# Decode step on one core: in the sample attention, a chunk's four transposes ahead of its score products, and seven load buffers

## The chip, the cores and the metric

The kernel is one program on one core of a Trainium2 chip. The metric is the device time of an execution in microseconds (us). The engines are TensorE (PE, with its weight loads as PEld), VectorE (DVE), ScalarE (ACT), GpSimd (POOL) and SyncE (SP). Here SP only issues DMA transfers, and POOL issues the gathers.

## The reference, cut to what matters

The program is one step of a hybrid layer for two groups that share all weights: a prompt of 1024 tokens and 8 samples of 4 new tokens with a past of 2048. The part that the change is about is the attention of the samples:

```python
def nsa_block(q, g, pos_q, ck, cv, kb, vb, kw, vw, pos_w):
    s = einsum(q, ck) * scale - slope * d_c          # compressed blocks
    o_c = masked_probs(s) @ cv
    _, idx = top_k(score, 16)                        # blocks of 64 rows
    ks, vs = kb[idx], vb[idx]                        # selected blocks
    o_s = masked_probs(einsum(q, ks) * scale - slope * d_s) @ vs
    o_w = masked_probs(einsum(q, kw) * scale - slope * d_w) @ vw   # last 512 rows
    return gate[0] * o_c + gate[1] * o_s + gate[2] * o_w

def memory_attend(mq, mkv):                          # 256 memory rows, 4 heads
    return softmax(mq @ k * scale) @ v

def merge(x, o_a, o_b, o_c, gb, w_o):
    return x + (concatenate([o_a, o_b, o_c]) * gb) @ w_o
```

Everything before and after it (projections, the prompt's own attention, the state space branch, the MLP) is the same in both kernels.

## The kernel before, in words

`run` (L129) builds the program in stages. The instructions of a stage are written in program order, and a scheduler in the framework then fixes the order on every engine before the program runs. It lays the stages over one another where tiles and buffers allow. On the chip each engine takes its instructions strictly in that order.

Three stages matter here. `nsa_keys` (L695) makes the prompt's keys: it loads `kd` and transposes it into `kps` (L735), loads the bias rows `augk` on POOL's queue (L725 to L727) and the rows `augq` on SP's (L705). `sample` (L1322) is the attention of the samples, and `nsa_prompt` (L741) the attention of the prompt. The last two run over one another on all engines: `sample` has the PSUM tag `sS` with two banks, `nsa_prompt` has `S` (three banks, the scores, L835 to L838), `T` (two, transposed probabilities, L889) and `O` (one, L903). For a unit of the prompt, `prep` (L774) makes QB on POOL from `augq` (L786). DVE finds the maximum of each score tile (L843) and scales the probabilities (L876); ACT takes the exponential (L844) and copies T out of PSUM (L891).

`sample` goes twice (Q = 0, 1) over four samples each. In each round it first scores the compressed blocks and ranks the blocks on DVE and POOL (L1446 to L1455). Then come five chunks: the window (c = 4) and the four quarters of the selected blocks (c = 0 to 3). A chunk needs four tiles `xs` (128x1024 f32, one per sample). For the window SP loads them; for the other chunks they are gathered by POOL's queue from `cache_slc_kv` (L1334). There are six `xs` buffers, so that while a chunk holds four, the next one can have two on the way. A chunk's steps are a product that puts the bias into its score bank S (L1489); for each of four groups a: four transposes of the keys (L1494), an evacuation to SBUF on ACT or DVE (L1343, L1345) and four score products (L1498); the maximum and the exponential (L1501, L1507); four transposes of the probabilities (L1517); and sixteen value products (L1523), after which the four `xs` are free. S is held all the while, so the transposes of a chunk have the other bank of `sS` alone. After the chunks a round ends with the memory part: eight tiles of keys and values from `cache_mem_kv` through the same `xs` buffers (L1332), eight groups of transposes and products (L1563, L1567), value products (L1584) and the gated result in `mixs`.

After both, `out_proj` (L1637) multiplies the mixed branches with `w_o` (L122 to L124 on `ops`), in the order of the tuple `ORDER = (4, 5, 6, 0, 7, 1, 8, ...)` of feature blocks. Blocks 4 to 11 are loaded from scratch (`mxr`), and split into a high and a low part on ACT and DVE (L112 `mxh`, L118 `mxl`). Their tiles lie in the SBUF space that `sample` leaves, and so can be made once it is done. The first weight block `w0` is loaded and split early, during `nsa_prompt`; the others (`raw` <- `w_o`, L1624) lie in the space that `nsa_prompt` and its keys leave.

Of the kernel before, what the change touches and what calls it, by code (L numbers as in the profile page):

```python
# [8 lines left out]
F32 = mybir.dt.float32  # L9
R32 = mybir.dt.float32r  # L10
BF16 = mybir.dt.bfloat16
# [3 lines left out]
ALU = mybir.AluOpType  # L15
# [86 lines left out]
class Build:  # L102
# [593 lines left out]
    def nsa_keys(self, pool):  # L696
        nc, A = self.nc, self.A
# [6 lines left out]
        self.augq = pool.tile([128, 1032], F32, name="augq")  # L704
        nc.sync.dma_start(self.augq[64:128], A["c_augq"])  # L705
# [64 lines left out]
    def nsa_units(self, pool, psp, j, g):  # L770
        nc = self.nc
        ctx = {"n": 0, "total": (j + 1) + min(j + 1, 5) + 1}

        def prep():  # L774
            tk = slice(j * 128, j * 128 + 128)
            qd = pool.tile([128, 4, 128], F32, name="qd", tag="qd", bufs=3)
            for dd in range(2):
                nc.sync.dma_start(qd[dd * 64:(dd + 1) * 64], self.s_q[g * 256:(g + 1) * 256, tk].rearrange("(h d) t -> d h t", d=64))
            qd = qd.rearrange("p h t -> p (h t)")
            if g == 0:  # L780
                self._gn = pool.tile([128, 3, 8], F32, name="gn", tag="gn", bufs=2)
                nc.sync.dma_start(self._gn.rearrange("p b h -> p (b h)"), self.s_gn[tk])
            ctx["gn"] = self._gn
            QA = pool.tile([128, 512], R32, name="QA", tag="QA", bufs=2)
            QB = pool.tile([128, 512], R32, name="QB", tag="QB", bufs=2)
            nc.gpsimd.tensor_scalar(QB[64:128], self.augq[64:128, g * 512:(g + 1) * 512], self.augq[64:128, 1024 + j:1025 + j], None, op0=ALU.mult)  # L786
            nc.scalar.activation(QA, qd, AF.Copy, scale=0.125)
            nc.vector.scalar_tensor_tensor(QB[0:64], qd[0:64], 0.125, QA[0:64].bitcast(F32), op0=ALU.mult, op1=ALU.subtract)
            ctx["QA"], ctx["QB"] = QA, QB
            ctx["gb"] = pool.tile([128, 256], F32, name="ngb", tag="ngb", bufs=5)  # L790
            for a in range(2):
                nc.sync.dma_start(ctx["gb"][:, a * 128:(a + 1) * 128], self.s_gb[2 * g + a][:, j * 128:(j + 1) * 128])

        return [self.nsa_unit(pool, psp, j, g, b, ctx, prep if b == 0 else None, b == (0 if j < 7 else 1)) for b in range(2)]
# [524 lines left out]
    def sample(self, pool, psp):  # L1319


        nc, A = self.nc, self.A  # L1322
# [6 lines left out]
        def load(src, q="sync", idx=None):  # L1329
            t = pool.tile([128, 4, 256], F32, name="xs", tag="xs", bufs=6)  # L1330
            if idx is None:
                nc.sync.dma_start(t, src)  # L1332
            else:
                nc.gpsimd.indirect_dma_start(out=t.rearrange("n l f -> n (l f)"), out_offset=None, in_=src,  # L1334
                                             in_offset=bass.IndirectOffsetOnAxis(ap=idx, axis=0))
            return t
# [71 lines left out]
        for Q in range(2):  # L1408
# [33 lines left out]
            cm = [pool.tile([128, 4, 256], F32, name="xs", tag="xs", bufs=6).rearrange("p a b -> p (a b)")[:, :900].rearrange("p (j i) -> p j i", i=30)  # L1442
# [27 lines left out]
            PT = pool.tile([128, 512], F32, name="sPT", tag="sPT", bufs=3)  # L1470
# [8 lines left out]
            for c in (4, 0, 1, 2, 3):  # L1479
# [8 lines left out]
                S = psp.tile([128, 512], F32, name="sS", tag="sS", bufs=2)  # L1488
                nc.tensor.matmul(S, sta[:, c], mov[:, int(c == 4)], start=True, stop=False, skip_group_check=True)  # L1489

                for a in range(4):
                    pt = pst()
                    for bb in range(4):
                        nc.tensor.transpose(pt[:, bb * 128:(bb + 1) * 128], xs[bb][:, a, 0:128], ident)  # L1494
                    KT_ = pool.tile([128, 512], F32, name="KTs", tag="KTs", bufs=3)
                    evac(KT_, pt)
                    for bb in range(4):
                        nc.tensor.matmul(S[BR[bb]:BR[bb] + 32, a * 128:(a + 1) * 128], Qb[:, Q * 4 + bb], KT_[:, bb * 128:(bb + 1) * 128],  # L1498
                                         start=False, stop=True, skip_group_check=True)
# [6 lines left out]
                P = pool.tile([128, 512], F32, name="sP", tag="sP", bufs=2)  # L1506
# [11 lines left out]
                PT = pool.tile([128, 512], F32, name="sPT", tag="sPT", bufs=3)  # L1518
# [36 lines left out]
            ps = psp.tile([128, 512], F32, name="sS", tag="sS", bufs=2)  # L1555
# [3 lines left out]
            for h in range(4):  # L1559
                for l in range(2):  # L1560
# [3 lines left out]
                    MK = pool.tile([128, 512], F32, name="KTs", tag="KTs", bufs=3)  # L1564
                    evac(MK, pt)
                    for bb in range(4):
                        nc.tensor.matmul(ps[BR[bb]:BR[bb] + 32, l * 128:(l + 1) * 128], Qm[:, Q * 4 + bb, h], MK[:, bb * 128:(bb + 1) * 128],  # L1567
                                         start=h == 0 and l == 0, stop=h == 3, skip_group_check=True)
            xv = [part(bb, 512) for bb in range(4)]
            PM = pool.tile([128, 512], F32, name="sP", tag="sP", bufs=2)  # L1570
# [8 lines left out]
            PT = pool.tile([128, 512], F32, name="sPT", tag="sPT", bufs=3)  # L1579
# [254 lines left out]
```

## Time and profile before

| | |
|---|---|
| median of 3 runs | 2028.8 us (2024.67 to 2034.67) |
| the profiled execution | 2028.2 us, its span 2026.4 us |
| PE busy in the span | 1912.8 us (94%) |
| DVE, ACT, POOL busy | 1154.9, 756.7, 434.4 us |
| DMA | 191.44 MB, 94 GB/s on average |

The page gives the busy time of each engine over the whole span, and the busy tenths in 40 slices of some 51 us each. An engine that is busy is not an engine at its best: a matmul that runs at half the clock is busy for twice as long. The row PEclk gives the granted clock of TensorE as a share of full speed (0.5 is 1.2 GHz, 1.0 is 2.4 GHz). The sample attention and the prompt attention lie between 640 and 1096 us.

### The profile page before, as it was taken

The numbers are of one execution on the slowest core, as the hardware profiler recorded it, in microseconds if no ns is written. First come the engines' busy times: TensorE is split into PE (matmuls) and PEld (weight loads), VectorE is DVE, ScalarE is ACT, GpSimd is POOL, SyncE is SP. The second block draws the span as 40 slices with busy tenths as digits, with TensorE's granted clock in tenths as the row PEclk, the third lists the DMA queues.
The fourth block names the chain that finished last, engine by engine and source line by source line (L and its number), as shares of the span: only waits on it lengthen the run. The fifth ranks groups of instructions, "written<-read, shape, count | busy, mean of one in ns | idle before, by whom it ended". The sixth has DMA issues, their size and how long they took to land.

```text
span 2026.4 us, 33851 instructions
## 1 busy us (share of the span) xinstructions
PE 1912.8 (94%) x13280; PEld 1727.5 (85%) x13280; DVE 1154.9 (57%) x2759; ACT 756.7 (37%) x1696; POOL 434.4 (21%) x281
## 2 busy tenths in 40 slices
PE   8998999999997999999987999799999999999997
PEld 8987889999996665656545999799999999999997
DVE  6387995425536777787653225745554555554535
ACT  6301224226645676667643224122222211122222
POOL 2043431441112211011100122422211211122200
PEclk9998999999997899999996999899999999999999
DMA  7453334563345533232226222211111111111102
GB/s 266 147 138 87 99 92 111 177 214 126 126 129 143 160 96 117 84 106 71 90 93 190 74 70 62 62 51 44 53 53 42 46 49 43 42 43 52 42 1 86
DMA packets 197609, 191.44 MB, mean 94 GB/s; under 512 B 32845, under 2 KB 176966, under 8 KB 196234
## 3 DMA queue, kind: packets, MB, share of 16 engines
q1 hardware_dynamic: 190730, 154.13, 25.5%
q0 software_dynamic: 6720, 35.16, 5.1%
q8 instruction: 104, 1.70, 0.4%
q14 instruction: 55, 0.45, 0.1%
HBM read 155.34 MB, written 38.55 MB: 96 GB/s over the span
## 4 chain that ended last, share of the span: by engine, by line
PE 51%; DMA 2%; DVE 2%; issue 1%; ACT 1%; SPq 0%; DVEq 0%; POOL 0%; ACTq 0%; POOLq 0%
PE fps L122 12%; PE fps L124 12%; PE fps L123 12%; PE ops L122 2%; PE ops L123 2%; PE ops L124 2%; PE O L903 2%; PE T L889 2%; DMA xs<-cache_slc_kv,idx 1%; PE S L838 1%; PE S L835 1%; PE sS L1494 1%; DMA raw<-w_o 1%; DVE acc L1717 0%; PE xps L1651 0%
## 5 line engine op out<-in xcount | busy, mean ns | idle before, releaser
L1761 DVE TENSOR_TENSOR acc<-fps,acc 128x352 f32<-128x352 f32 (+3 forms) x360 | 185.1, 522 | 156.5 <-PE fps L124 156.5
L123 PE MATMUL fps<-h2lo,hi 128*128 128x352 f32 x768 | 248.6, 324 | 2.0 <-DVE h2lo L1705 2.0
L122 PE MATMUL fps<-h2hi,hi 128*128 128x352 f32 x768 | 248.2, 324 | 1.9 <-ACT h2hi L1704 1.9
L123 PE MATMUL fps<-yl,f2hi 128*128 128x352 f32 (+3 forms) x768 | 246.3, 323 | 3.3 <-DVE yl L1738 3.3
L124 PE MATMUL fps<-h2hi,lo 128*128 128x352 f32 x768 | 249.1, 324 | 0.0
L122 PE MATMUL fps<-yh,f2hi 128*128 128x352 f32 (+3 forms) x768 | 242.6, 325 | 6.0 <-DVE rm L1753 6.0
L124 PE MATMUL fps<-yh,f2lo 128*128 128x352 f32 (+3 forms) x768 | 245.9, 323 | 0.0
L1736 DVE TENSOR_TENSOR rl<-rl 128x352 f32<-128x352 f32 x96 | 132.2, 1378 | 146.1 <-ACT rl L1735 146.1
L118 POOL TENSOR_TENSOR lo<-raw,hi 128x1024 fp32r<-128x1024 f32 (+1 forms) x43 | 96.8, 2252 | 359.1 <-ACT hi L112 359.1
L124 PE MATMUL pso<-hhi,wlo 128*128 128x352 f32 x480 | 157.3, 328 | 0.0
L123 PE MATMUL pso<-hlo,whi 128*128 128x352 f32 x480 | 157.3, 328 | 0.0
L122 PE MATMUL pso<-hhi,whi 128*128 128x352 f32 x480 | 157.2, 328 | 0.0
L118 POOL TENSOR_TENSOR f2lo<-raw,f2hi 128x1024 fp32r<-128x1024 f32 x32 | 79.1, 2474 | 361.6 <-ACT f2hi L112 348.5
L843 DVE TENSOR_REDUCE nst<-S 128x1 f32<-128x384 f32 (+4 forms) x264 | 108.9, 433 | 80.2 <-PE S L838 59.5
L122 PEld LDWEIGHTS fps<-yh,f2hi 128*128 128x128 f32 x768 | 144.0, 189 | 7.8 <-DVE rm L1753 6.3
L123 PEld LDWEIGHTS fps<-yl,f2hi 128*128 128x128 f32 x768 | 144.8, 189 | 5.0 <-DVE yl L1738 3.6
L123 PEld LDWEIGHTS fps<-h2lo,hi 128*128 128x128 f32 x768 | 145.4, 189 | 2.3 <-DVE h2lo L1705 2.3
L122 PEld LDWEIGHTS fps<-h2hi,hi 128*128 128x128 f32 x768 | 145.2, 189 | 2.2 <-ACT h2hi L1704 2.2
L124 PEld LDWEIGHTS fps<-h2hi,lo 128*128 128x128 f32 x768 | 146.1, 190 | 0.0
L124 PEld LDWEIGHTS fps<-yh,f2lo 128*128 128x128 f32 x768 | 144.8, 189 | 1.4
L844 ACT ACTIVATE P<-S,nst 128x384 f32<-128x384 f32 (+4 forms) x264 | 127.4, 489 | 33.3 <-DVE nst L843 29.1
L112 ACT ACTIVATE f2hi<-raw 128x1024 fp32r<-128x1024 f32 x32 | 33.8, 1059 | 282.6 <-PE fps L123 268.7
(593 smaller groups left out, 4535.5 us busy)
## 6 DMA issues: line engine op xcount, KB each, us to landing
raw<-w_ff SPq DMA_DIRECT2D x64, 512.0 KB
wraw<-w_in SPq DMA_DIRECT2D x28, 512.0 KB
xs<-cache_mem_kv SPq DMA_DIRECT2D x16, 512.0 KB
s_gb<-st SPq DMA_DIRECT2D x36, 176.0 KB
x<-x_prompt SPq DMA_DIRECT2D x8, 512.0 KB
wraw<-w_mem_kv SPq DMA_DIRECT2D x8, 512.0 KB
qd<-s_q SPq DMA_DIRECT2D x32, 128.0 KB
ngb<-s_gb SPq DMA_DIRECT2D x64, 64.0 KB
```

The lines of the kernel that those rows point to most:

```text
L112: nc.scalar.activation(hi, src, AF.Copy)
L118: eng.tensor_tensor(lo, src, hi.bitcast(F32), op=ALU.subtract)
L122: mm(ps, ahi, bhi, start=start, stop=False)
L123: mm(ps, ahi, blo, start=False, stop=False)
L124: mm(ps, alo, bhi, start=False, stop=stop)
L835: nc.tensor.matmul(S[:, :w], ctx["QA"][:, qs], KA[:, k0:k0 + w], start=True, stop=False)
L843: nc.vector.tensor_reduce(t[:, 0, pi, i:i + 1], S[:, o:o + pw], axis=AX.X, op=ALU.max, negate=True)
L844: nc.scalar.activation(P[:, o:o + pw], S[:, o:o + pw], AF.Exp, bias=t[:, 0, pi, i:i + 1], accum_out=t[:, 1, pi, i:i + 1])
L889: nc.tensor.transpose(T[:w, i * 128:(i + 1) * 128], Ps[i, si][:, o:o + w], self.ident)
L903: nc.tensor.matmul(O[c * 64:(c + 1) * 64, :256], v, pv[:w, c], start=n == 0, stop=n == total - 1)
L1736: tt(r, r, r, op=ALU.mult)
L1761: tt(acc[:, m, o:o + n], ps[:, :n], acc[:, m, o:o + n], op=ALU.add)
```

## The change

Three things change in `sample`, and one in `nsa_keys` that makes room for them.

1. A chunk first does all four groups of transposes, each into its own `KTs` tile (four instead of three), and only then takes the score bank, puts the bias in and does its sixteen score products in one burst. The memory part does the same in two halves of four groups.
2. There are seven `xs` buffers instead of six.
3. `sPT` has two buffers instead of three and `sP` one instead of two.
4. `augq` is kept as bf16, and is loaded by POOL's queue; its last eight columns become a small tile `augj` of their own, loaded by SP.

```diff
-        self.augq = pool.tile([128, 1032], F32, name="augq")
-        nc.sync.dma_start(self.augq[64:128], A["c_augq"])
+        self.augq = pool.tile([128, 1024], BF16, name="augq")
+        nc.gpsimd.dma_start(self.augq[64:128], A["c_augq"][:, 0:1024])
+        self.augj = pool.tile([128, 8], F32, name="augj")
+        nc.sync.dma_start(self.augj[64:128], A["c_augq"][:, 1024:1032])
...
-            t = pool.tile([128, 4, 256], F32, name="xs", tag="xs", bufs=6)
+            t = pool.tile([128, 4, 256], F32, name="xs", tag="xs", bufs=7)
...
-                S = psp.tile([128, 512], F32, name="sS", tag="sS", bufs=2)
-                nc.tensor.matmul(S, sta[:, c], mov[:, int(c == 4)], start=True, stop=False, skip_group_check=True)
-
+
+                KT_ = []
                 for a in range(4):
                     pt = pst()
                     for bb in range(4):
                         nc.tensor.transpose(pt[:, bb * 128:(bb + 1) * 128], xs[bb][:, a, 0:128], ident)
-                    KT_ = pool.tile([128, 512], F32, name="KTs", tag="KTs", bufs=3)
-                    evac(KT_, pt)
+                    KT_.append(pool.tile([128, 512], F32, name="KTs", tag="KTs", bufs=4))
+                    evac(KT_[a], pt)
+                S = psp.tile([128, 512], F32, name="sS", tag="sS", bufs=2)
+                nc.tensor.matmul(S, sta[:, c], mov[:, int(c == 4)], start=True, stop=False, skip_group_check=True)
+                for a in range(4):
                     for bb in range(4):
-                        nc.tensor.matmul(S[BR[bb]:BR[bb] + 32, a * 128:(a + 1) * 128], Qb[:, Q * 4 + bb], KT_[:, bb * 128:(bb + 1) * 128],
+                        nc.tensor.matmul(S[BR[bb]:BR[bb] + 32, a * 128:(a + 1) * 128], Qb[:, Q * 4 + bb], KT_[a][:, bb * 128:(bb + 1) * 128],
                                          start=False, stop=True, skip_group_check=True)
...
-                P = pool.tile([128, 512], F32, name="sP", tag="sP", bufs=2)
+                P = pool.tile([128, 512], F32, name="sP", tag="sP", bufs=1)
...
-                PT = pool.tile([128, 512], F32, name="sPT", tag="sPT", bufs=3)
+                PT = pool.tile([128, 512], F32, name="sPT", tag="sPT", bufs=2)
...
-            for h in range(4):
-                for l in range(2):
+            ps = None
+            for h0 in (0, 2):
+                MK = []
+                for h, l in ((h0, 0), (h0, 1), (h0 + 1, 0), (h0 + 1, 1)):
...
+                ps = ps or psp.tile([128, 512], F32, name="sS", tag="sS", bufs=2)
+                for h, l, mk in MK:
```

The lines of the changed kernel are two further down from L705 on, three or more further from L1487 on (L1494, L1498 and L1523 are L1495, L1502 and L1527 there).

**Place 1: PE, behind the value products of the first gathered chunk (Q = 0, c = 0).** `xs` numbers tell the four tiles of the next chunk apart. Before, the next chunk's bias product and other scores follow, then transposes of its first two tiles:

```order
L1527 MATMUL sS_7541<-VN_7314,PN_7375 32x128 x4
...
L1494 MATMUL sS_7574<-ident_103,xs_7564 128x128
L1494 MATMUL sS_7574<-ident_103,xs_7566 128x128
L835 MATMUL S_9560<-KA01_6815,QA_9476 128x448
...
L838 MATMUL S_9560<-KB01_6819,QB_9477 128x448
L1494 MATMUL sS_7574<-ident_103,xs_7568 128x128
L903 MATMUL O_9606<-PT_9597,V0_6838 64x256 x2
...
L838 MATMUL S_9570<-KB01_6819,QB_9477 128x448
L1494 MATMUL sS_7574<-ident_103,xs_7570 128x128
```

In the changed kernel the same place reads:

```order
L1531 MATMUL sS_7543<-VN_7316,PN_7377 32x128 x4
L1495 MATMUL sS_7574<-ident_103,xs_7566 128x128
L1495 MATMUL sS_7574<-ident_103,xs_7568 128x128
L1495 MATMUL sS_7574<-ident_103,xs_7570 128x128
L905 MATMUL O_9372<-PT_9380,cvp_111 64x256 x2
...
L1495 MATMUL sS_7581<-ident_103,xs_7566 128x128
L1495 MATMUL sS_7581<-ident_103,xs_7568 128x128
L1495 MATMUL sS_7581<-ident_103,xs_7570 128x128
L837 MATMUL S_9461<-KA10_6818,QA_9345 128x384
...
L1495 MATMUL sS_7574<-ident_103,xs_7572 128x128
```

Three transposes now stand right behind the value products, the second group's first three come ahead of the first group's fourth, and only the fourth tile is one whose gather had to wait for the value products. Before, that held for the third and the fourth tile.

**Place 2: PE, at the end of the attention.** Before, the whole memory part of Q = 1 stands behind the last product of the prompt attention (`O<-PT,cvp`), of which the end is this; `out_proj` begins with `g2r`:

```order
L1563 MATMUL sS<-ident,xs 128x128 x4
L1567 MATMUL sS<-KTs,Qm 32x128 x4
L1578 MATMUL sS<-ident,sP 128x128 x2
L1584 MATMUL sS<-xs,sPT 32x512 x8
L1591 MATMUL sS<-ident,os 128x128
L237 MATMUL xps<-ident,g2r 128x8
L1651 MATMUL xps<-ident,xr 128x128 x8
L122 MATMUL ops<-mxh_12903,w0hi 128x352 x3
```

In the changed kernel the last transpose of the samples (L1598) stands 196 matmuls of the prompt attention ahead of that product, and behind the product there is this:

```order
L905 MATMUL O<-PT,V_6841 64x256 x2
L905 MATMUL O<-PT,cvp 64x256 x2
L237 MATMUL xps<-ident,g2r 128x8
L122 MATMUL ops<-mxh_12905,w0hi 128x352
L123 MATMUL ops<-mxl_12906,w0hi 128x352
L124 MATMUL ops<-mxh_12905,w0lo 128x352
```

Nothing of `sample` is left behind the prompt attention. 27 products with `w0` come first (blocks 4, 5 and 6), then those with the next weight block.

**Place 3: ACT, in the last part of the prompt attention.** Before, all splits of loaded blocks stand behind the last copy of T. In the changed kernel eight splits from scratch lie among the exponentials and copies of the prompt attention, of which this is the beginning:

```order
L893 ACTIVATE PT<-T 128x512
L112 ACTIVATE mxh_12905<-mxr 128x1056
L112 ACTIVATE mxh_12921<-mixs 128x4x32
L846 ACTIVATE P,nst<-S,nst 128x512
L846 ACTIVATE P,nst<-S,nst 128x64
L893 ACTIVATE PT<-T 128x512
L112 ACTIVATE mxh_12911<-mxr 128x1056
L846 ACTIVATE P,nst<-S,nst 128x512
L893 ACTIVATE PT<-T 128x512 x2
L112 ACTIVATE mxh_12917<-mxr 128x1056
```

The splits moved from behind the attention into it; DVE has their second halves (L118) in the same places, and SP their eight loads ahead of the first `raw` <- `w_o`.

## Rows read from the trace of the kernel before

**Rows 1.** The page, 40 slices of the span: granted clock of TensorE in tenths

```profile
PEclk9998999999997899999996999899999999999999
```

**Rows 2.** Windows; us, busy of PE, PEld, DVE, ACT, POOL, PEclk, DMA share, GB/s

```profile
700.00:1053.20 353.20, 335.27 (x2742) 212.16 (x2745) 250.35 (x804) 240.75 (x728) 48.77 (x39) 0.99 0.29 88
```

**Rows 3.** Windows from the end of the prompt attention into out_proj

```profile
1053.20:1096.20 43.00, 22.38 (x160) 11.84 (x159) 17.92 (x40) 11.09 (x16) 0.00 (x0) 0.57 0.66 203
1096.20:1106.20 10.00, 8.97 (x46) 8.03 (x45) 1.54 (x2) 4.25 (x7) 0.00 (x0) 0.81 0.51 174
1106.20:1116.20 10.00, 10.00 (x63) 9.93 (x64) 3.76 (x4) 2.86 (x4) 0.00 (x0) 1.00 0.49 160
```

**Rows 4.** Timeline of PE and SP there; start, us, line, operation, count

```profile
1049.81 0.66 PE L889 MATMUL T<-ident,P 128*128 128x128 f32 x4
1050.39 0.65 PE L903 MATMUL O<-PT,V 128*64 128x256 f32 x4
1050.97 0.65 PE L889 MATMUL T<-ident,P 128*63 128x128 f32 x4
...
1052.57 0.65 PE L903 MATMUL O<-PT,cvp 63*64 63x256 f32 x4
...
1054.71 2.67 SPq L1332 DMA_DIRECT2D xs<-cache_mem_kv  x4
...
1095.83 1.23 PE L122 MATMUL ops<-mxh,w0hi 128*128 128x352 f32 x3
```

**Rows 5.** The chain of waits there; start, us, what

```profile
1057.43 10.16 DMA raw<-w_o
1067.61 1.06 ACT hi L112
...
1073.17 6.45 DMA mxr<-s_mix
...
1098.21 4.81 DMA xr<-x_prompt
```

**Rows 6.** Waits of PE, 640 to 1215 us; us in total, times, longest

```profile
PE sS L1494 <- DMA xs<-cache_slc_kv,idx: 9.3, 8, 2.5
...
PE O L903 <- issue: 2.4, 1, 2.4
...
PE sS L1494 <- issue: 1.4, 1, 1.4
```

**Rows 7.** Timeline of PE around two sets of value products and late tiles

```profile
719.53 1.08 PE L1523 MATMUL sS<-xs,sPT 128*32 128x128 f32 x32
...
726.52 0.33 PE L1494 MATMUL sS<-ident,xs 128*128 128x128 f32 x1 [1.79 <-DMA xs<-cache_slc_kv,idx]
...
789.03 1.08 PE L1523 MATMUL sS<-xs,sPT 128*32 128x128 f32 x32
...
799.48 0.33 PE L1494 MATMUL sS<-ident,xs 128*128 128x128 f32 x1 [1.30 <-DMA xs<-cache_slc_kv,idx]
```

**Rows 8.** Windows of 20 us in the attention, columns as in Rows 2

```profile
720.00:740.00 20.00, 18.21 (x149) 10.71 (x140) 13.18 (x41) 12.42 (x38) 5.65 (x5) 0.91 0.50 152
...
780.00:800.00 20.00, 18.70 (x158) 11.91 (x156) 15.15 (x45) 14.96 (x46) 5.15 (x4) 1.00 0.44 137
...
880.00:900.00 20.00, 18.39 (x121) 10.99 (x119) 17.77 (x57) 13.25 (x43) 4.80 (x4) 1.00 0.52 174
```

**Rows 9.** Groups by line; busy us and mean ns | idle before, releaser

```profile
L843 DVE TENSOR_REDUCE nst<-S 128x1 f32<-128x384 f32 (+4 forms) x264 | 108.9, 433 | 80.2 <-PE S L838 59.5 <-ACT P L844 14.9 <-remote 2.9
L876 DVE TENSOR_SCALAR P<-P,nst 128x256 f32<-128x256 f32 (+4 forms) x264 | 80.4, 370 | 0.5
L118 DVE TENSOR_TENSOR mxl<-mxr,mxh 128x1024 fp32r<-128x1024 f32 (+1 forms) x12 | 14.6, 1233 | 23.5 <-ACT mxh L112 23.4
L112 ACT ACTIVATE mxh<-mxr 128x1024 fp32r<-128x1024 f32 (+1 forms) x12 | 12.7, 1065 | 17.4 <-DMA mxr<-s_mix 17.2 <-issue 0.2
```

**Rows 10.** Timeline of PE where the keys are transposed

```profile
609.67 0.66 PE L735 MATMUL kps<-ident,kd 128*128 128x128 f32 x4 [2.79 <-DMA kd<-s_kv]
```

More of the change, by code (lines that the diff above doesn't have):

```diff
@@ L785, in prep @@
             QB = pool.tile([128, 512], R32, name="QB", tag="QB", bufs=2)
-            nc.gpsimd.tensor_scalar(QB[64:128], self.augq[64:128, g * 512:(g + 1) * 512], self.augq[64:128, 1024 + j:1025 + j], None, op0=ALU.mult)
+            nc.gpsimd.tensor_scalar(QB[64:128], self.augq[64:128, g * 512:(g + 1) * 512], self.augj[64:128, j:j + 1], None, op0=ALU.mult)
             nc.scalar.activation(QA, qd, AF.Copy, scale=0.125)
@@ L1441, in sample @@
             nc.vector.tensor_reduce(imp, pi[:, :128].rearrange("p (j c) -> p j c", c=4), axis=AX.X, op=ALU.add)
-            cm = [pool.tile([128, 4, 256], F32, name="xs", tag="xs", bufs=6).rearrange("p a b -> p (a b)")[:, :900].rearrange("p (j i) -> p j i", i=30)
+            cm = [pool.tile([128, 4, 256], F32, name="xs", tag="xs", bufs=7).rearrange("p a b -> p (a b)")[:, :900].rearrange("p (j i) -> p j i", i=30)
                   for _ in range(2)]
@@ L1517, in sample @@
                     nc.tensor.transpose(pt[:, a * 128:(a + 1) * 128], P[:, a * 128:(a + 1) * 128], ident)
-                PT = pool.tile([128, 512], F32, name="sPT", tag="sPT", bufs=3)
+                PT = pool.tile([128, 512], F32, name="sPT", tag="sPT", bufs=2)
                 evac(PT, pt)
@@ L1553, in sample @@
                 tt(mixs[sl].rearrange("p (b t) -> p b t", t=4), pv[:, :, g, :, h], gbs[sl].rearrange("p (b t) -> p b t", t=4), op=ALU.mult)
-            ps = psp.tile([128, 512], F32, name="sS", tag="sS", bufs=2)
             src = [A["cache_mem_kv"][Q * 4 + bb].rearrange("(n l) f -> n l f", l=2) for bb in range(4)]
@@ L1563, in sample @@
                         nc.tensor.transpose(pt[:, bb * 128:(bb + 1) * 128], xk[bb][:, l, h * 128:(h + 1) * 128], ident)
-                    MK = pool.tile([128, 512], F32, name="KTs", tag="KTs", bufs=3)
-                    evac(MK, pt)
+                    MK.append((h, l, pool.tile([128, 512], F32, name="KTs", tag="KTs", bufs=4)))
+                    evac(MK[-1][2], pt)
+                ps = ps or psp.tile([128, 512], F32, name="sS", tag="sS", bufs=2)
+                for h, l, mk in MK:
                     for bb in range(4):
-                        nc.tensor.matmul(ps[BR[bb]:BR[bb] + 32, l * 128:(l + 1) * 128], Qm[:, Q * 4 + bb, h], MK[:, bb * 128:(bb + 1) * 128],
+                        nc.tensor.matmul(ps[BR[bb]:BR[bb] + 32, l * 128:(l + 1) * 128], Qm[:, Q * 4 + bb, h], mk[:, bb * 128:(bb + 1) * 128],
                                          start=h == 0 and l == 0, stop=h == 3, skip_group_check=True)
             xv = [part(bb, 512) for bb in range(4)]
-            PM = pool.tile([128, 512], F32, name="sP", tag="sP", bufs=2)
+            PM = pool.tile([128, 512], F32, name="sP", tag="sP", bufs=1)
             sm2 = pool.tile([128, 3], F32, name="sm2", tag="sm2", bufs=2)
@@ L1578, in sample @@
                 nc.tensor.transpose(pt[:, l * 128:(l + 1) * 128], PM[:, l * 128:(l + 1) * 128], ident)
-            PT = pool.tile([128, 512], F32, name="sPT", tag="sPT", bufs=3)
+            PT = pool.tile([128, 512], F32, name="sPT", tag="sPT", bufs=2)
             nc.vector.tensor_copy(PT[:, :256], pt[:, :256])
```

## The prediction, made before the changed kernel was run

> **What bounds the kernel now.** I read the page's slices first, then windows by stage, then the timeline and the waits inside the stages that the change touches. The clock row shows two dips in the first half of the span, in slices 13 and 14 and in slice 22, counted from one, and a shallow one in slice 26 [rows 1]. A slice is 50.7 us, so slice 22 begins at 1064 us: it holds the end of the attention, and there lies this change. Ahead of it, from 700 us to the end of the prompt attention, PE is busy 335 of 353 us at 0.99 of full clock: PE is the bound, and DVE (71%) and ACT (68%) follow it [rows 2]. Over the next 43 us PE is busy 22.4 us at 0.57 of the clock [rows 3]. That stretch is the memory part of the second round of samples, alone, with the first loads of `out_proj` beside it. The last product of the prompt attention ends at 1053.2, and the first product of `out_proj` starts at 1095.8 [rows 4].
>
> PE's loss inside the attention is small and has a pattern. After a chunk's value products its buffers come free, a gather is issued, and PE, which takes its order strictly, meets the transposes of the late tile too soon: 9.3 us in 8 waits for gathers, and 1.4 and 2.4 us in two idle times marked "issue" at two of these places [rows 6]. In four windows of 20 us that hold such waits the mean clock is 0.91 (the second of them is shown); a window with one wait of 1.3 us stays at 1.00 [rows 7, 8].
>
> **The change, part by part.**
>
> *The tail of the samples.* PE's order is fixed, and in the new one the samples end 196 prompt matmuls before the prompt attention does (place 2). The stretch from 1053.2 to full speed in `out_proj` is what can be saved. It is 1095.8 − 1053.2 = 42.6 us, plus what the next 10 us lose against the ten after them: 46 matmuls where 63 fit, so 2.7 us [rows 3, 4]. Together 45.3 us. What remains of it:
>
> - The memory part's work moves into the attention. PE was busy 22.4 us at 0.57 of the clock, so 12.8 us at full clock [rows 3]; less the last chunk's own value products, 1.0 us [rows 7], and eight transposes of the residual at 0.58 us for four [rows 4], 1.2 us, this leaves 10.6 us.
> - These eight transposes come later, but cost their 1.2 us all the same.
> - A new wait stands behind the end of the attention. PE has 27 products with `w0` there, 4.3 us at the 63 in 10 us of the full-speed window [rows 3]. The next need `raw` <- `w_o`, which SP can issue only when the attention's space is free. Before it was issued 4.2 us after that end, behind four memory loads of samples that took 2.7 us to issue [rows 4, 5]. I set 1.5 us, then 6.45 us for a load of the same 512 KB and 1.06 for the split's first half [rows 5], so 9.0 us. PE waits 9.0 − 4.3 = 4.7 us, and the half clock after it costs 1.8 us (below): 6.5 us. With the quickest such load, 4.8 us, it is 4.9 us, with the slowest, 10.2, it is 10.3 us [rows 5]. The slowest had four sample loads ahead of it that are gone; I take the middle one.
>
> 45.3 − 10.6 − 1.2 − 6.5 = **27.0 us saved** (23 to 29).
>
> *The waits for gathers.* Before: 9.3 + 1.4 + 2.4 = 13.1 us [rows 6]. Each of the four dips costs 0.09 of 20 us, 1.8 us [rows 8]: 7.2 us. Sum 20.3 us. After: with seven buffers three tiles of the next chunk are there already, and the order reaches the fourth later (place 1). I count what stands between the value products and that transpose: 0.145 us a transpose, 0.29 for a value product of the prompt (two records) [rows 4], and for a score product of n columns n × 0.45 ns, from 63 products of 352 columns in 10 us [rows 3]. For the eight gathered chunks this gives 3.7, 6.2, 6.2, 6.1 us (Q = 0) and 3.8, 5.8, 4.6, 6.1 us (Q = 1). Before, the third tile came after 3.6 to 7.8 us. The first gather lands some 6.0 us after the value products end (719.5 + 1.0 to 726.5); the one beside memory loads took 9.4 us (790.0 to 799.5) [rows 7]. With 6.0 us for seven and 9.4 for the last chunk of the first round the waits are 2.3 + 0 + 0 + 3.3 + 2.2 + 0.2 + 1.4 + 0 = 9.4 us. Three are as long as those that were followed by half clock: 5.4 us. Sum 14.8, so **5.5 us saved**. If all land 0.4 us sooner: 4.7 us and two dips, 12 saved. If all take 9.4 us: 32.7 us of waits and eight dips, 47 us, 27 lost. I take the value near the lower end: where the third tile came after 3.6 to 7.8 us, no wait before was longer than 2.5 us [rows 6].
>
> A dip follows the wait of 1.8 us, and none the wait of 1.3 us [rows 7, 8]. The Trainium skill (TensorE: Matmul & The Clock Gate, "HAM oscillation — how this bites in real kernels") warns of a loop in which a DMA wait at every tile makes every tile start cold. [...]
>
> *The splits of `mxr`.* Eight of them now lie in the last part of the prompt attention (place 3): 8 × 1.065 us on ACT and 8 × 1.233 on DVE [rows 9]. That part is some 37 us of PE work by the prices above. DVE has there some 26 maxima and 32 scalings, 11.3 + 11.8 us, 3 us of small operations and these 9.9 us [rows 9]: 36 us, as much as PE. Before, this work lay beside `out_proj`, where PE was the bound, and cost nothing; that cover is gone. Where DVE was busy 17.8 of 20 us, PE did 121 matmuls where other windows do about 150 [rows 8], some 4 us lost. For twice that length, with PE work to spare in the queue of T and O, I charge **6 us** (0 if the waits interleave, 12 if the splits' loads hold ACT and DVE up as well).
>
> *The keys.* Without the 258 KB of `augq` ahead of it on SP's queue the scheduler expects `kd` sooner, and puts its first transposes four transposes and five products of 256 columns earlier. The bytes are moved either way, and PE waited 2.8 us for `kd` already [rows 10]. The work that was done before this wait is now behind it: 0.6 + 5 × 0.12 = 1.2 us at full clock, 2.4 at half. I take **2 us lost** (0 to 5, the upper end with a second dip, and with the six `augk` transfers one place later on POOL's queue).
>
> *Nothing:* the evacuations (same number and size; two banks take turns, and PE has other work between), the later score bank (maximum and exponential have over 3 us of prompt products to hide under), bf16 for `augq` (the same elements through the same POOL operation), fewer `sP` and `sPT` (the next writer comes a chunk later).
>
> **Sum**, against the profiled execution of 2028.2 us (0.6 below the median of the runs): 2028.2 − 27.0 − 5.5 + 6 + 2 = 2003.7; on the median's scale **2004 us**.
>
> **The rivals.**
>
> 1. *The gathers take it back.* If tiles land as late as beside memory loads in most chunks, or the fourth tile's transposes are reached some 2 us sooner than counted, each chunk waits about 3 us and pays a dip: 24 + 14.4 = 38 us in place of 14.8, so 2004 + 23 = 2027 us, no change. For it: PE met a late tile in eight waits already [rows 6]. Against it: the order has 4 to 6 us of work there, and one gather in eight was the slow one.
> 2. *The splits' loads become the bound, slower than before.* Each load needs its scratch buffer back from the split before. If they go one after another (6.45 + 1.06 + 1.23 = 8.7 us each [rows 5, 9]), seven take 61 us where the last part has 43 with its losses; ACT and DVE hold the prompt's work behind them, and SP holds the weight load behind the last one. That is 18 us in place of 6: 2016. It turns slower than before from some 10.5 us a load and split (73.5 us in all, 30.5 lost). With loads of 9.4 us, as the slow gather, it is 11.7 us, 82 in all, 39 lost in place of 6: 2037 us. Against it: two buffers take turns, which halves it, and DMA is at 0.29 of its time in the attention [rows 2].
> 3. *More than the sum.* No wait of the fourth tile, splits that fit: 2004 − 9 − 6 = 1989 us. For it: PE is at 95% in the attention with all its waits [rows 2]; against it: DVE's load in the last part.
> 4. *It doesn't do what it says.* The end of the samples ahead of the prompt attention is in the order of the program, so I give this none of its own.
>
> **How the numbers follow.** Forecast 0.68, rival 1 0.13, rival 2 0.05, rival 3 0.14. Half a per cent, 10 us, is about what a measurement can tell from no change. The forecast and rival 3 are faster by more than that, except for the forecast's own upper end (23 for the first term, 12 us for the splits, 5 for the keys, nothing from the gathers: 2022), which I give 0.04: faster 0.78. Rival 1 and that end: same 0.17. Rival 2: slower 0.05. The range goes from 1990, which leaves out about half of rival 3, to 2026, which takes in the forecast's upper end and about half of rival 1.
>
> **What would show it.** Right: the waits of L1567 and L1563 after the prompt attention are gone; PE's half-clock stretch behind it is under 10 us instead of 43, and the last product of the prompt attention ends near 1066 us. The waits of the fourth transposes sum to 9 us, three of them over 2. DVE's idle time in the last 44 us of the attention is nearly nil. Wrong: gather waits above 20 us (rival 1); ACT waiting for `mxr` by more than 12 us inside the attention (rival 2); a `kps` wait above 6 us; or a prompt attention that ends after 1075 us for another reason.

## The result, and the profile after

The changed kernel takes 2001.1 us (median of four runs, 2000.1 to 2002.4) beside 2030.0 us for the kernel before, run with it (four runs, 2024.7 to 2034.7). The ratio is 0.986, 95% interval 0.9843 to 0.9877. The prediction was 2004 us, with a range from 1990 to 2026. The profiled execution has a span of 1999.8 us, 26.6 less than the one before.

Windows of the changed kernel, in the columns of [rows 2] (us, then busy of PE, PEld, DVE, ACT, POOL, then the granted clock, DMA share, GB/s). The first two are the stretches of [rows 2, 3], then come two windows of 20 us inside the attention, the last 44 us of the attention, and the first 10 us of `out_proj`:

```profile
700.00:1053.20 353.20, 336.00 (x2841) 220.97 (x2838) 263.72 (x831) 247.23 (x739) 47.28 (x38) 0.97 0.36 109
1053.20:1096.20 43.00, 39.02 (x239) 32.84 (x238) 13.33 (x30) 13.54 (x23) 0.00 (x0) 0.96 0.39 120
740.00:760.00 20.00, 14.14 (x112) 10.27 (x110) 12.01 (x36) 9.60 (x28) 6.97 (x6) 0.83 0.52 146
840.00:860.00 20.00, 15.58 (x104) 10.55 (x100) 17.34 (x50) 10.73 (x36) 5.56 (x3) 0.83 0.24 80
1022.20:1066.20 44.00, 38.70 (x250) 20.77 (x248) 31.11 (x87) 33.75 (x83) 0.00 (x0) 1.00 0.26 82
1066.20:1076.20 10.00, 7.93 (x41) 7.33 (x42) 3.52 (x6) 3.35 (x4) 0.00 (x0) 0.88 0.80 258
```

The stretch that had PE busy for 22.4 of 43 us at 0.57 of the clock now has 39.0 at 0.96. It holds the end of the prompt attention and the first products of `out_proj`. The price stands in the other rows: 0.97 of the clock from 700 us on instead of 0.99, two windows at 0.83, and a last part of the attention in which PE is busy for 38.7 of 44 us.

PE around the end of the attention (timeline: start, us, line, operation, count), which answers to [rows 4]:

```profile
1065.55 0.65 PE L905 MATMUL O<-PT,cvp 63*64 63x256 f32 x4 [0.16 <-ACT PT L893]
1066.28 0.43 PE L122 MATMUL ops<-mxh,w0hi 128*128 128x352 f32 x1
```

The chain of waits there (start, us, what), which answers to [rows 5]:

```profile
1067.54 4.31 DMA raw<-w_o
1071.87 1.07 ACT hi L112
1072.98 0.43 PE ops L122
```

The last prompt product ends at 1066.2 us and `out_proj` starts 0.1 us later. PE's 27 products with `w0` cover all of the load of `raw` and its split but 2.1 us. Waits of PE from 640 to 1100 us (total, times, longest), which answer to [rows 6]:

```profile
PE S L837 <- ACT P L846: 7.0, 6, 3.4
PE S L840 <- POOL QB L788: 6.6, 2, 5.9
PE O L905 <- ACT PT L893: 6.1, 9, 1.6
PE ops L122 <- ACT hi L112: 2.1, 1, 2.1
PE sS L1495 <- DMA xs<-cache_slc_kv,idx: 1.8, 4, 0.6
```

The waits for gathers fell from 9.3 us in eight to 1.8 in four. Two others took their place. The kernel before has no wait for QB; here there are 6.6 us, 5.9 of them in one. Waits of scores for the exponential grew from 1.3 to 7.0 us.

The long wait for QB shows a mechanism that the prediction did not see. The first two rows are POOL, the last two PE (timeline, idle time before a row in brackets):

```profile
745.29 0.94 POOL L1336 DMA_INDIRECT xs<-cache_slc_kv,idx  x1 [0.30 <-PE S L840]
753.08 3.22 POOL L788 TENSOR_SCALAR QB<-augq,augj 64x512 fp32r<-64x512 bf16 x2 [6.85 <-issue]
...
748.64 0.20 PE L839 MATMUL S<-mkb,idb 128*128 128x64 bf16 x1
754.70 0.63 PE L840 MATMUL S<-KB,QB 128*128 128x320 f32 x1 [5.86 <-POOL QB L788]
```

POOL issues the fourth gather at 745.3 us and then stands still for 6.85 us before QB, although nothing runs on it. The order of the program with its waits says why. DMASW is the completion of a transfer that POOL issued:

```
L1336 DMA xs_7736<-cache_slc_kv,idx4_7260 128x1024 [waits DMASW3_49,PE_49]
L788 TENSOR_SCALAR QB_9734<-augq_6812,augj_6814 64x512 [waits DMASW4_49,DMASW2_49,DMASW5_49,DMASW1_49,DMASW6_49,DMASW0_49,DMASW7_49,DVE_49,PE_49]
L788 TENSOR_SCALAR QB_9921<-augq_6812,augj_6814 64x512 [waits DVE_49,PE_49]
```

A QB that stands behind gathers on POOL waits until they have landed. In the kernel before this is so as well, as a row of POOL's waits shows (total, times, longest):

```profile
POOL QB L786 <- DMA xs<-cache_slc_kv,idx: 10.7, 2, 6.1
```

But there no product of PE met a QB that was not ready. In the new order two do, and the clock of the window around the longer wait falls to 0.83.

The second window at 0.83, from 840 to 860 us, has another cause. POOL and DVE rank the blocks of the second round there, and one small operation of DVE lasts until POOL's ranking operation ends (timeline):

```profile
850.04 2.66 POOL L1449 TENSOR_TENSOR xs<-xs,tri 128x900 f32<-128x900 f32 x1 [11.49 <-DVE xs L1448]
850.88 1.85 DVE L869 TENSOR_TENSOR nfy<-nfy 128x4 f32<-128x4 f32 x1
853.71 0.69 PE L837 MATMUL S<-KA,QA 128*128 128x384 f32 x1 [3.37 <-ACT P L846]
```

The same operation takes 0.16 us on average in the last part of the attention. Maxima of scores stand behind it and two ranking operations on DVE, ACT's exponential waits for them, and PE waits 3.4 us for the exponential.

### The profile page after: what moved, and what is told of

It is laid out like the page before. It is cut to its first block, busy times and chain, and to the rows that moved or that the text cites. A ratio compares the mean times of both kernels' runs of the same rounds, so it can differ in the third digit from the quotient of the medians.

```text
span 1999.8 us, 33859 instructions
## 1 busy us (share of the span) xinstructions
PE 1898.9 (95%) x13280; PEld 1727.9 (86%) x13280; DVE 1154.1 (58%) x2759; ACT 756.6 (38%) x1696; POOL 434.3 (22%) x282
## 4 chain that ended last, share of the span: by engine, by line
PE 82%; DVE 7%; DMA 4%; issue 3%; ACT 2%; SPq 1%; POOL 1%; DVEq 0%; ACTq 0%; POOLq 0%
PE fps L122 12%; PE fps L124 12%; PE fps L123 12%; PE pso L122 4%; PE pso L124 4%; PE pso L123 4%; PE O L905 4%; PE T L891 4%; PE ops L122 2%; PE ops L124 2%; PE ops L123 2%; PE S L840 2%; PE S L837 2%; PE cps L630 1%; PE cps L122 1%
## 5 line engine op out<-in xcount | busy, mean ns | idle before, releaser
L118 POOL TENSOR_TENSOR lo<-raw,hi 128x1024 fp32r<-128x1024 f32 (+1 forms) x43 | 97.0, 2256 | 369.9 <-ACT hi L112 367.0
L118 POOL TENSOR_TENSOR f2lo<-raw,f2hi 128x1024 fp32r<-128x1024 f32 x32 | 79.6, 2487 | 363.1 <-ACT f2hi L112 354.9
L112 ACT ACTIVATE f2hi<-raw 128x1024 fp32r<-128x1024 f32 x32 | 33.8, 1059 | 284.3 <-PE fps L123 269.1
```

The costliest lines, as they stand in the source:

```text
L118: eng.tensor_tensor(lo, src, hi.bitcast(F32), op=ALU.subtract)
```

## The experiments

Each variant is built by the same scheduler, so an edit in one place can move other instructions too. Where that matters, the text names what moved. Ratios are to runs of the kernel before on the same chip.

**x1: the burst with six buffers**

```diff
-            t = pool.tile([128, 4, 256], F32, name="xs", tag="xs", bufs=7)
+            t = pool.tile([128, 4, 256], F32, name="xs", tag="xs", bufs=6)
```

> The changed kernel with six xs buffers instead of seven; the burst order stays. In PE's order the samples still end ahead of the prompt attention, by 52 prompt matmuls instead of 196. Theory (the burst order ends the lone tail, the seventh buffer only saves waits for gathers): no half-clock stretch behind the attention, first ops matmul within 5 us of the attention's end, and the third and fourth tile of a chunk wait again, 5 to 10 us in all plus their dips of the clock; 2004 to 2014 us. Rival A (the seventh buffer makes the gain): 2022 us or more. Rival B (the seventh buffer gives nothing): 2001 us, gather waits under 3 us.

Measured: 2002.6 us, ratio 0.9886 (0.9855 to 0.9918), not to be told from the changed kernel's 0.986. The waits for gathers and for QB (as above):

```profile
PE sS L1495 <- DMA xs<-cache_slc_kv,idx: 6.4, 7, 1.7
PE S L840 <- POOL QB L788: 0.3, 1, 0.3
```

The gather waits are those of the theory (6.4 us in seven), the time lies just under its range and near rival B's. Here PE waits 4.6 us more for gathers than in the changed kernel and 6.3 us less for QB; its idle time in the attention is 35.0 us against 35.3. So with QB on POOL the seventh buffer exchanges one wait for another. Rival A is out.

**x2: seven buffers, old order of the samples**

```diff
 (with the room edits of x3)
-            t = pool.tile([128, 4, 256], F32, name="xs", tag="xs", bufs=6)
+            t = pool.tile([128, 4, 256], F32, name="xs", tag="xs", bufs=7)
```

> Seven xs buffers with everything that makes room for them (augq as bf16, sP and sPT one fewer), but the order of transposes and score products of the kernel before. In PE's order 72 sample matmuls still stand behind the prompt attention's end (92 before). Theory: the tail of the samples stays, some 35 us of it at half clock, and only the gather waits fall, from 9.3 us to 3 to 6: 2015 to 2026 us. Rival A (the seventh buffer makes the gain): 2008 us or less.

Measured: 2025.2 us, ratio 1.0003 (0.9985 to 1.0022): no difference. Waits, and a window behind the end of the attention at 1063.8 us:

```profile
PE S L840 <- POOL QB L788: 10.6, 3, 6.0
PE sS L1496 <- DMA xs<-cache_slc_kv,idx: 3.9, 3, 2.3
```

```profile
1060.00:1080.00 20.00, 14.38 (x109) 7.77 (x108) 9.28 (x20) 7.56 (x11) 0.00 (x0) 0.66 0.95 296
```

The tail is there, as the theory has it: 14.4 of 20 us busy at 0.66 of the clock, and the first `ops` only at 1092.6 us. The gather waits fell to 3.9 us, and 10.6 us of waits for QB are new. With QB on POOL the seventh buffer alone brings nothing; the burst order makes the gain.

**x3: the edits that make room, alone**

```diff
-        self.augq = pool.tile([128, 1032], F32, name="augq")
-        nc.sync.dma_start(self.augq[64:128], A["c_augq"])
+        self.augq = pool.tile([128, 1024], BF16, name="augq")
+        nc.gpsimd.dma_start(self.augq[64:128], A["c_augq"][:, 0:1024])
+        self.augj = pool.tile([128, 8], F32, name="augj")
+        nc.sync.dma_start(self.augj[64:128], A["c_augq"][:, 1024:1032])
...
-  tag="sPT", bufs=3    tag="sP", bufs=2
+  tag="sPT", bufs=2    tag="sP", bufs=1
```

> The kernel before with only the edits that make room: augq as bf16 on POOL's queue, one sP, two sPT. Order of the samples as before. Theory (the keys cost some 2 us, the fewer score buffers nothing): 2024 to 2034 us, the wait of the keys' transposes for kd 5 to 7 us instead of 4.1, the rest of the waits as before. Rival: the fewer buffers or the keys cost over 10 us: 2040 us.

Measured: 2031.2 us, ratio 1.0029 (1.001 to 1.0048), so 2 to 10 us slower than the 2026.6 us of the kernel before beside it. That overlaps the 0 to 5 us of the prediction; the place does not fit: the keys' transposes wait 4.6 us for `kd`, hardly more than the 4.1 before. There is a new wait of 2.6 us for QB, but the profiled execution is the fastest of the ten, with a span of 2026.3 us beside 2026.4 for the kernel before. So where the loss lies is not shown.

**x4: the burst in the chunks only, the memory part in the old order**

```diff
-            for h0 in (0, 2):
-                MK = []
-                for h, l in ((h0, 0), (h0, 1), (h0 + 1, 0), (h0 + 1, 1)):
+            ps = psp.tile([128, 512], F32, name="sS", tag="sS", bufs=2)
+            for h in range(4):
+                for l in range(2):
...
```

> The changed kernel with the memory part in the old order (each group's transposes followed by its products, score bank held throughout); the chunks keep the burst. In PE's order the samples end 200 prompt matmuls ahead of the prompt attention's end (196 in the changed kernel). Theory (what counts is that the samples end first, and the chunks' burst does that): 1997 to 2006 us. Rival (the memory part's burst matters, since its products otherwise wait for evacuations inside the attention as they did in the tail, 8.9 us there): 2008 to 2012 us, with KTs waits of 5 us or more.

Measured: 2016.0 us, ratio 0.9948 (0.9928 to 0.9967), slower than the changed kernel by 15 us (medians) or 18 (ratios). Neither side is right. The samples do end ahead of the prompt, and PE waits 0.3 us for KTs in all; but the edit in the memory part changed the order elsewhere:

```profile
PE S L840 <- POOL QB L788: 12.4, 3, 6.2
PE sS L1495 <- DMA xs<-cache_slc_kv,idx: 5.9, 4, 2.8
```

```profile
1041.00:1085.30 44.30, 38.55 (x224) 20.84 (x222) 28.04 (x79) 29.62 (x73) 0.00 (x0) 0.88 0.22 69
```

Waits for QB are 12.4 us instead of 6.6, those for gathers 5.9 instead of 1.8, and the last 44 us of the attention run at 0.88 of the clock. In the profiled execution (2021.0 us, the slowest of its seven) the attention is 21.6 us longer than in the changed kernel: PE is idle for 10.5 us more of it, and busy for 11.1 us more with the same 3430 products, at 0.92 of the clock instead of 0.94. So waits and clock have about half each. Whether the memory part's burst is worth anything by itself stays open, since the edit moved the rest of the order too.

**x5 and x6: QB on another engine**

```diff
-            nc.gpsimd.tensor_scalar(QB[64:128], self.augq[64:128, g * 512:(g + 1) * 512], self.augj[64:128, j:j + 1], None, op0=ALU.mult)
x5
+            nc.vector.tensor_scalar(QB[64:128], self.augq[64:128, g * 512:(g + 1) * 512], self.augj[64:128, j:j + 1], None, op0=ALU.mult)
x6
+            nc.scalar.activation(QB[64:128], self.augq[64:128, g * 512:(g + 1) * 512], AF.Copy, scale=self.augj[64:128, j:j + 1])
```

> The changed kernel with the bias product QB made by DVE instead of POOL. On POOL each QB that stands behind gathers waits in the program for the landing of those gathers; on DVE it does not. Theory (this wait is the new cost of the changed kernel: 6.6 us of waits of PE for QB in its trace, and a window of 20 us at 0.83 of the clock beside the longest): waits for QB under 1 us, 1988 to 1996 us. Rival A (something else holds PE at these places, or DVE's sixteen more operations cost as much): 1998 to 2005 us. Rival B (the gathers' own waits come back, since PE now meets them earlier): gather waits above 6 us, 1996 to 2004 us.

> As x5, with QB made by ACT. Theory: the same as on DVE within 4 us, 1987 to 1998 us, since neither engine is full outside the last 44 us. Rival (the engine that takes it becomes late: ACT holds the exponentials and copies of the prompt): waits of PE for ACT above 20 us in the attention instead of 14, over 2000 us.

Measured: x5 2004.6 us, ratio 0.9878 (0.9853 to 0.9904); x6 1985.9 us, ratio 0.9785 (0.9762 to 0.9808). In both orders QB no longer waits for gathers, and neither trace has a wait of PE for QB. The window 840 to 860 us of x5, in which the ranking for the second round lies:

```profile
840.00:860.00 20.00, 13.19 (x74) 9.59 (x71) 18.54 (x53) 7.29 (x26) 4.59 (x3) 0.76 0.25 79
```

x5 has the time of its rival A: the window with the long wait for QB is at full clock now, but in this one DVE is busy 18.5 of 20 us and PE 13.2 at 0.76. The ranking on POOL holds a small operation of DVE for 1.85 us here as in the changed kernel, so how much of the loss is QB's work on DVE is not shown. x6 missed the first half of its theory, since it differs from x5 by 19 us and not by 4; its time is just better than the range of 1987 to 1998, and its rival is out. The same window and the waits of x6:

```profile
840.00:860.00 20.00, 18.86 (x157) 12.13 (x155) 17.86 (x63) 14.94 (x45) 1.87 (x2) 1.00 0.35 107
```

```profile
PE O L905 <- ACT PT L893: 5.7, 9, 1.3
PE S L837 <- ACT P L846: 3.3, 6, 0.8
PE sS L1495 <- DMA xs<-cache_slc_kv,idx: 0.7, 1, 0.7
```

PE is busy 18.9 us there at full clock, the gather waits are 0.7 us, and the waits for ACT's exponential fell from 7.0 to 3.3 us although ACT has more to do. The kernel is 15 us faster than the changed one, and the intervals of the two ratios do not touch. Not all of this need be the wait for QB. The order of x6 also puts the ranking elsewhere, so that DVE takes maxima of scores beside POOL's operation, and nothing is held there (three maxima in 1.0 us):

```profile
835.31 2.63 POOL L1449 TENSOR_TENSOR xs<-xs,tri 128x900 f32<-128x900 f32 x1 [72.14 <-PE T L891]
836.10 1.01 DVE L845 TENSOR_REDUCE nst<-S 128x1 f32<-128x384 f32 x3
```

Every window of 20 us of x6 from 680 to 1020 us is at full clock. How the 15 us divide between QB and the ranking was not tried apart.

**x7: x2 with QB on DVE**

```diff
-            nc.gpsimd.tensor_scalar(QB[64:128], ...
+            nc.vector.tensor_scalar(QB[64:128], ...
```

> x2 (seven buffers, old order) with QB on DVE. In x2 the waits for gathers fell from 9.3 to 3.9 us, and waits for QB rose from 0 to 10.6 us. Theory (the seventh buffer moved PE's wait from the gathers to QB, and is worth something once QB does not wait): 2008 to 2018 us, waits for QB under 1 us, 47 sample matmuls left behind the attention instead of 72. Rival (the seventh buffer is worth nothing because the tail takes back what the attention gains): 2020 us or more.

Measured: 2007.3 us, ratio 0.9902 (0.9866 to 0.9938), 18 us faster than x2. There is no wait for QB and none for a gather. The attention ends at 1055.8 us (x2: 1063.8) and the first `ops` comes at 1076.4 (1092.6). Against x11 below (old order, six buffers, QB on ACT, ratio 0.9982) it is 0.8% faster. So the seventh buffer was worth something in x2 as well, and QB's wait hid it. These two differ in the engine of QB too, so the size is rough; and 8.2 us of what x7 gains on x2 lie behind the attention, where fewer products of the samples are left (47 instead of 72).

**x8: the second halves of the splits on POOL**

```diff
-            self.split(self.mhi[f][:, :n], self.mlo[f][:, :n], raw[:, :n], e_lo="dve")
+            self.split(self.mhi[f][:, :n], self.mlo[f][:, :n], raw[:, :n], e_lo="dve" if pool else "pool")
```

> The changed kernel with the second halves of the eight splits from scratch on POOL, which is idle in the last 44 us of the attention, instead of DVE. Theory (these splits are what holds PE there: 38.7 of 44 us busy, with the engines behind the scores late): PE busy 41 us or more of the last 44, DVE about 10 us less, 1996 to 1999 us. Rival A (DVE had room left, 31.1 of 44 us, so its splits cost nothing): 2000 to 2002 us. Rival B (POOL takes twice as long for one, holds the two load buffers and makes the first products of out_proj wait): 2003 us or more.

Measured: 2008.0 us, ratio 0.9896 (0.9864 to 0.9927), 7 us slower than the changed kernel by the medians; the intervals of the two ratios overlap a little. Two groups of DVE in the last part of the attention (count, busy us and mean ns), first in the changed kernel, then here:

```profile
L845 DVE TENSOR_REDUCE nst<-S 128x1 f32<-128x512 f32 x8 | 5.5, 688 | 3.1 <-PE S L840 2.9
L878 DVE TENSOR_SCALAR P<-P,nst 128x512 f32<-128x512 f32 x8 | 3.3, 484 | 0.0
```

```profile
L878 DVE TENSOR_SCALAR P<-P,nst 128x512 f32<-128x512 f32 x8 | 7.2, 972 | 0.0
L845 DVE TENSOR_REDUCE nst<-S 128x1 f32<-128x512 f32 x8 | 5.3, 688 | 2.8 <-PE S L840 2.8
```

DVE lost eight splits of 1.24 us and was as busy as before over the last 44 us (31.7 us against 31.1). The scalings of probabilities in SBUF took 972 ns instead of 484, one of them 2584, about as long as a split on POOL (2435); the maxima of scores in PSUM kept their 688 ns. Most of these eight maxima ran while POOL stood still, but one of 384 and two of 256 columns that ran beside a split kept their time too (0.56 and 0.42 us). For the scalings the timeline shows both cases, a group of six with POOL idle and another group of six beside a split:

```profile
1031.86 1.93 DVE L878 TENSOR_SCALAR P<-P,nst 128x384 f32<-128x384 f32 x6
1061.32 4.04 DVE L878 TENSOR_SCALAR P<-P,nst 128x384 f32<-128x384 f32 x6
1061.79 2.50 POOL L118 TENSOR_TENSOR mxl<-mxr,mxh 128x1024 fp32r<-128x1024 f32 x1 [2.10 <-ACT mxh L112]
```

Rival B's time came by a way that no theory named: out_proj did not wait longer (2.2 us), DVE did while POOL worked, and PE did 226 products in the last 44 us instead of 250, at 0.92 of the clock. The Trainium skill (SBUF — State Buffer, "Who interferes with whom") says that DVE and GpSimd share a pair of SBUF ports as an exclusive lock, which a `tensor_scalar` within SBUF can need and a `tensor_reduce` never does; these rows agree.

**x9: four of the eight splits back behind the attention**

```diff
-                self.mix_split(pool if k < 4 else None, (k,), NT if k in (6, 7) else NP)
+                self.mix_split(pool if k < 4 or k > 7 else None, (k,), NT if k in (6, 7) else NP)
```

> The changed kernel with the loads of blocks 8 to 11 into buffers that are free only after the attention, so that four of the eight splits from scratch stand behind the prompt attention again (ACT, DVE and SP), where PE has products to do. Theory (eight splits cost about 6 us in the last part, so four of them 3): PE busy over 40 of the last 44 us of the attention instead of 38.7, 1996 to 1999 us. Rival A (ACT with 33.8 and DVE with 31.1 of 44 us had room, the splits cost nothing): 2000 to 2003 us. Rival B (these loads now stand beside the weights' and out_proj waits for them): waits of ops for ACT above 5 us instead of 2.1, 2003 us or more.

Measured: 1996.3 us, ratio 0.9842 (0.9818 to 0.9866). The last 44 us of the attention:

```profile
1017.30:1061.30 44.00, 40.77 (x267) 22.22 (x266) 27.92 (x89) 32.66 (x86) 0.00 (x0) 1.00 0.15 44
```

PE is busy for 40.8 us instead of 38.7, and `out_proj` waits 2.3 us where it waited 2.1. The last part is as the theory has it; the time agrees (4.8 us by the medians), but its interval overlaps that of the changed kernel, so the time alone does not show it. The attention as a whole is 7.4 us shorter, so most of the difference lies ahead of this stretch, and is not shown to be the splits'.

**x10: x6 and x9 together**

> x6 (QB on ACT) with the later loads of x9. In x6 the last 35 us of the attention have ACT and DVE at 16 to 18 of 20 us and two windows at 0.89 and 0.94 of the clock. Theory: these windows go to full clock, 1980 to 1984 us. Rival A: as x6, 1985 to 1990 us. Rival B (out_proj waits for the blocks): 1990 us or more.

Measured: 1982.6 us, ratio 0.9782 (0.9762 to 0.9802), the fastest here and not to be told from x6 by time. The end of the attention in x10 and in x6:

```profile
1000.00:1043.50 43.50, 41.48 (x276) 23.18 (x274) 29.09 (x91) 32.99 (x86) 0.00 (x0) 1.00 0.16 48
```

```profile
1012.50:1056.50 44.00, 39.85 (x239) 21.46 (x238) 29.10 (x83) 31.80 (x78) 0.00 (x0) 0.92 0.25 83
```

The clock of the last part is 1.00 instead of 0.92 in these two executions, as the theory has it. But the profiled execution is the fastest of four in x10 (1977.4 us) and the slowest of four in x6 (1990.6), so part of this may be chance.

**x11: the kernel before with QB on ACT**

```diff
-            nc.gpsimd.tensor_scalar(QB[64:128], self.augq[64:128, g * 512:(g + 1) * 512], self.augq[64:128, 1024 + j:1025 + j], None, op0=ALU.mult)
+            nc.scalar.activation(QB[64:128], self.augq[64:128, g * 512:(g + 1) * 512], AF.Copy, scale=self.augq[64:128, 1024 + j:1025 + j])
```

> The kernel before with QB on ACT and nothing else. Its trace has no wait of PE for QB, and 100 sample matmuls stand behind the attention (92 before). Theory (QB costs only where the new order meets it too soon): no difference, 2024 to 2034 us. Rival (POOL's QB slows DVE wherever it runs, or delays the gathers behind it): 2020 us or less.

Measured: 2021.6 us, ratio 0.9982 (0.9967 to 0.9997). That is 1 to 7 us faster, between theory and rival. QB on ACT is worth a few us by itself and some 15 in the changed kernel, where the order runs into it.

**x12: x6 with six buffers**

> x6 with six xs buffers. With seven buffers and QB on POOL the gain of the seventh was hidden by the waits for QB (x1 2002.6 us against 2001.1). Theory (with QB on ACT the seventh buffer is worth its gather waits, 6.4 us in x1 against 0.7 in x6): gather waits 4 to 8 us, 1990 to 1998 us. Rival (the seventh buffer is worth nothing in either): 1984 to 1989 us.

Measured: 2007.8 us, ratio 0.9919 (0.9887 to 0.9951), against 0.9785 in x6. With QB on ACT the seventh buffer is worth some 1.3% of the time, and the intervals do not touch. That is more than the theory gave, though the gather waits, 3.3 us against 0.7, stayed under its 4 to 8; so they are not where most of it lies. The profiled execution (span 1998.6) was the fastest of its four, and its attention is 12.9 us longer than that of x6, 7.7 of it idle time of PE. Why the other runs took up to 2018 us is open.

## Why the prediction was right, point by point

**The tail** went as forecast. From the end of the attention to the last product of `out_proj` it was 193.6 us before and is 153.6 now, 40.0 less. The prediction's terms give 45.3 − 1.2 − 6.5 = 37.6. The difference is in the wait for `raw`: its load took 4.3 us, less than the quickest of the range (4.8), where I had set 6.45, so PE waited 2.1 us and not 4.7. The attention ended at 1066.2 us, forecast was 1066. The half clock behind it cost little: 10 us at 0.88.

**The attention in sum** came out near too, by parts that were not all right. From the first keys' transpose to the last prompt product it took 443.6 us before and takes 453.7 now, 10.2 more, forecast were 10.6 − 5.5 + 6 + 2 = 13.1. PE's busy time in it grew by 7.3 us and its idle time from 32.5 to 35.3. The first keys' transpose comes 2.8 us later than before, and 2.5 of these were there already at a projection at 210 us, far ahead of the change. So −40.0 + 10.2 + 2.8 = −27.0, and the spans differ by 26.6.

- *The gather waits* were mis-sized. I expected 9.4 us and three dips, and 1.8 us came. The step that failed is the landing time of 6.0 us after the value products, 9.4 beside memory loads. Both held a late start of POOL, 0.8 us, where it is 0.3 in the first case below. Two late tiles for which PE did wait, so that its start marks the landing (POOL's issue, then PE's transposes):

```profile
692.88 1.15 POOL L1336 DMA_INDIRECT xs<-cache_slc_kv,idx  x1 [7.85 <-PE sS L1527]
...
697.45 0.44 PE L1495 MATMUL sS<-ident,xs 128*128 128x128 f32 x2 [0.57 <-DMA xs<-cache_slc_kv,idx]
...
771.89 0.99 POOL L1336 DMA_INDIRECT xs<-cache_slc_kv,idx  x1 [15.59 <-PE sS L1527]
...
779.03 0.44 PE L1495 MATMUL sS<-ident,xs 128*128 128x128 f32 x2 [0.51 <-DMA xs<-cache_slc_kv,idx]
```

  The first landed 4.6 us after its issue and 4.8 after the end of the value products (692.6), the second, beside memory loads, 7.1 and 7.9 (771.1). PE also came to these tiles 0.6 and 1.3 us later than the order's products add up to. Nor does each longer wait pay a dip: the kernel before has one in the window with a wait of 1.8 us, but in x9 the window of 20 us with a wait of 1.9 us (760 to 780 us) is at full clock.
- *The wait for QB* was missing. The prediction asked what stands behind the gathers on PE, and not what stands behind them on POOL. Waits for QB (6.6 us) and for the exponentials (5.7 us more, with one of 3.4 at the ranking), with two windows at 0.83 of the clock, took back what the gather waits gave: PE's idle time hardly changed. Two errors of opposite sign made the sum right, and that part of the hit was luck. x6 shows that some 15 us were to be had from both together.
- *The splits* were right in sign and near in size. PE lost 44 − 38.7 = 5.3 us in the last 44 us, against 44 − 42.4 = 1.6 in the last 44 of the kernel before, so 3.7 us where 6 were charged; x9 gave 2.1 us back for four of the eight, and that the other four make up the rest is argued, not shown. But DVE was busy for 31 of these 44 us and not without idle time as I wrote; ACT was the fuller one with 33.8. x8 adds that DVE's share is not freed by giving it to POOL.
- *The keys*: waits for `kd` rose from 4.1 to 5.9 us, yet the last of these transposes starts 11.4 us after the first instead of 11.6. The 2 us lay inside the range, and x3, whose waits for `kd` hardly grew, leaves open where the loss of the room edits lies.

**The rivals.** Rival 1 was right that something in the attention takes the gain of the gathers back, and wrong in what: it was POOL's program and the ranking, not the landing. Rival 2 did not come: in the last 44 us the waits of ACT for `mxr` were 2.9 us. Rival 3 had the gathers nearly right (1.8 us of waits) and missed QB and the ranking, as the forecast did.

A slip of the reading changes no term: slice 22 of [rows 1] lies behind the middle of the span, so only one of the two dips is in its first half.

## What to carry to other kernels

When a change brings transfers forward, look at the queue that issues them. What stands behind them there may wait for their landing, and a wait that PE loses in one place can then come back in another, here about as long. Before work is given to an idle engine, ask which ports and waits it shares: here the kernel was 15 us faster with the same product on ACT than with it on POOL, and no faster with it on DVE.

## What was not expected of the hardware

A split on POOL slowed DVE to half speed in some operations and left others as they were: 972 against 484 ns for the scalings of 512 columns within SBUF, 0.56 and 0.42 us as ever for the maxima of 384 and 256 columns that read PSUM (x8). In the changed kernel an operation of DVE on 128x4 elements within SBUF took 1.85 us instead of 0.16 beside POOL's ranking. A gather of one 512 KB tile landed 4.6 us after its issue, and 7.1 us beside loads of memory rows, both quicker than the kernel before had led me to count.
